# When the second layer's memory keys are split, in a two-layer hybrid encoder on one core

## The chip, the cores and the metric

The kernel runs on one core of one Trainium2 chip. The metric is the device time of one execution in microseconds. The kernel before takes 899.92 us (median of three runs, 897.84 to 900.17).

## What is computed

Two encoder layers over x of 256 x 2048. Each layer multiplies x by one wide input projection, runs three groups of heads, gates them and multiplies by an output projection; all in float32. The part that matters here is the memory attention and the two projections that follow its key projection in the program:

```python
h = x @ w_in
a_q, a_k, a_v, a_z, b_q, b_k, b_v, b_z, b_lr, m_q, m_z = jnp.split(h, cuts, axis=-1)
y_a = chunk_band_attention(heads_a(a_q), heads_a(a_k), heads_a(a_v), rel_table)
...
o_b = gla_chunk_recurrence(heads_k(b_q), heads_k(b_k), heads_v(b_v), heads_k(log_g))
...
mkv = mem @ w_mem_kv                      # mem: 256 tokens x 2048
mk, mv = jnp.split(mkv, 2, axis=-1)
y_m = memory_attention(heads_m(m_q), heads_m(mk), heads_m(mv))
...
y = jnp.concatenate([y_a * silu(a_z), y_b * silu(b_z), y_m * silu(m_z)], axis=-1)
x = layer_norm(DEEPNORM_ALPHA * x + y @ w_out, ln_g, ln_b)
```

## The kernel before

**Products in two parts.** A large product keeps float32 accuracy by splitting both operands into a rounded high part and the rest: `parts` (lines 126 to 129) rounds with a copy on ACT (ScalarE, line 128) and subtracts the rounded from the raw value on DVE (VectorE, line 129). PE (TensorE) then adds three products, high x high, low x high and high x low (`as_products`, lines 258 to 264).

**Weight pieces.** A projection of 512 columns (`as_group`, line 266) is done in 8 pieces of 256 rows. For each piece (`piece`, lines 140 to 158) SP issues the DMAs into `raw`, ACT makes `wh`, DVE makes `wl`, and PE does 12 matmuls of 512 columns. `raw`, `wh` and `wl` have 4 buffers each: the load of a piece waits until DVE has made the `wl` of the piece four places earlier, and a cast until PE is done with that piece.

**Turning.** Some results are needed with rows and columns exchanged. `turned` (from line 520) transposes 32 x 32 blocks on DVE (line 525), writes them to DRAM with a DMA issued by POOL (GpSimd; `home<-sc`, line 527), and two ticks later reads them back with 8 DMAs of POOL that put the blocks in place (`qk<-home`, line 532). What is then done to the turned tile is written in a `place` function, which `laid_out` hands to `placed`.

**Order of the work.** PE, SP and POOL run in the order of the program. After each 512-column piece `tick` moves a clock on by 1 and runs the generators on the list `side` whose time has come; a side generator that `laid_out` registers with 9 thus issues its instructions behind the ninth piece after the turning. On ACT and DVE a scheduler at build time orders the instructions, but the `place` instructions are pinned (`placed_here`): they keep their place in the program. Each engine takes its instructions one after the other, so one that waits holds all behind it.

**The place of the edit.** In the second layer the memory's values and keys (`G_MV`, `G_MK`) are projected first. The keys `acc` are turned into `raw` (a tile of the tag `qk`); then come the 8 pieces of `G_BQK` (queries and keys of the linear attention, line 863), `gla_inputs`, and `values(0, 512)`, a further 8 pieces (line 889). The `place` of the keys does two `parts` calls, so two casts on ACT and two subtractions on DVE, into `mk[0]` and `mk[1]`. They are read by `m_head` late in the layer. The result of `G_BQK` is turned in the same way, and lines 860 and 861 place it 9 pieces after that (`gq` on ACT, `gk` on DVE). Between the weight pieces DVE also scales and shifts the residual of the first layer (`restored`, lines 660 and 661, `res`).

Of the kernel before, what the change touches and what calls it, by code (L numbers as in the profile page):

```python
# [31 lines left out]
G_MK, G_MV, G_BQK, G_AQ0, G_AK0, G_AQ1, G_AK1, G_MQ, G_BZ, G_AZ0, G_AZ1, G_MZ, G_WO = range(13)  # L32
# [4 lines left out]
def hybrid_trunk_kernel(  # L37
# [12 lines left out]
    waiting, active, side, done, now, linear = [], [], [], set(), [0], []  # L50

    def tick(share=1.0):

        now[0] += share
        for e in [e for e in side if e[1] <= now[0]]:
            side.remove(e)
            after = next(e[0], None)
            if after is not None:
                side.append((e[0], now[0] + after))
            else:  # L60
                done.add(e[0])
        while True:
            while waiting and len(active) < (3 if all(g in done for g in linear) else 2):
                active.append((waiting.pop(0), 0))
            due = [e for e in active if e[1] <= now[0]]
            if not due:
                return
            active.remove(due[0])
            g = due[0][0]
            after = next(g, None)  # L70
            if after is not None:
                active.append((g, now[0] + after))
                return
            done.add(g)

    def finish(gens):
        while not all(g in done for g in gens):
            tick()
# [18 lines left out]
    def nm(s):  # L97
        uid[0] += 1
        return f"{s}_{uid[0]}"
# [17 lines left out]
    def operand():  # L117

        x = opp.tile([P, 4, 2, T], F32R, name=nm("x"), tag="x")
        return x[:, :, 0], x[:, :, 1], x.rearrange("p j h t -> p j (h t)")  # L120
# [5 lines left out]
    def parts(hi, lo, src, keep=lambda ins: ins):  # L126

        keep(act.copy(hi, src))  # L128
        keep(dve.tensor_tensor(lo, src, hi.bitcast(F32), op=ALU.subtract))  # L129

    def load_quarter(src):

        with tc.high_priority(AHEAD):
            raw = wp.tile([P, 4, T], F32, name=nm("raw"), tag="raw")
            x = operand()
            sp.dma_start(raw, src)
            parts(x[0], x[1], raw)
        return x

    def piece(src, n, kp=2, home=None):  # L140

        with tc.high_priority(AHEAD):
            raw = wp.tile([P, kp, n], F32, name=nm("raw"), tag="raw")
            if home is None:
                hi, lo = (wp.tile([P, kp, n], F32R, name=nm(w), tag=w) for w in ("wh", "wl"))
            else:
                hi, lo = home
            if isinstance(src, list):
                at = 0
                for part in src:  # L150
                    if len(part.shape) == 2:
                        part = part.rearrange("p (k n) -> p k n", k=kp)
                    sp.dma_start(raw[:, :, at:at + part.shape[2]], part)
                    at += part.shape[2]
            else:
                sp.dma_start(raw.rearrange("p k n -> p (k n)"), src)
            parts(hi, lo, raw)
        return hi, lo

    def resident_quarter(q, src):  # L160

        with tc.high_priority(AHEAD):
            x = operand()
            sp.dma_start(early[:, q], src)
            parts(x[0], x[1], early[:, q])
        return x
# [91 lines left out]
    def as_products(o, t, xq, w, kt, kk, first=0):  # L258
        wh, wl = w
        xh, xl, _ = xq[kt // 4]  # L260
        j, ts = kt % 4, slice(t * P, (t + 1) * P)
        mm(o, xh[:, j, ts], wh[:, kk], kt == first, False)
        mm(o, xl[:, j, ts], wh[:, kk], False, False)
        mm(o, xh[:, j, ts], wl[:, kk], False, kt == 15)

    def as_group(src, xq, n, kp=2, first=None, need={}):

        acc = psd.tile([P, 2, 512], F32, name=nm("acc"), tag="acc")
        for pc in range(16 // kp):
            if first is not None and pc % 2 == 0:  # L270
                xq.append(load_quarter(first[pc // 2]))
            finish(need.get(pc, ()))
            w = piece(src[pc], n, kp)
            for kk in range(kp):
                for t in range(2):
                    as_products(acc[:, t, :n], t, xq, w, pc * kp + kk, kk)
            tick(n / 512)
        return acc
# [232 lines left out]
    def placed(raw, place):  # L511

        if place is not None:
            for t in range(2):
                place(raw[:, t].rearrange("p a (g j) -> p g a j", j=32),
                      lambda x: x[:, :, t * P:(t + 1) * P].rearrange("p g (a j) -> p g a j", j=32))
        return
        yield

    def turned(n, *todo, order="p b (g j) -> p g b j"):  # L520

        homes = []
        for _, src in todo:
            blocks = scratch([P, 4, n])
            dve.transpose(blocks.rearrange(order, j=32), src.rearrange("p (g b j) -> p g b j", b=4, j=32))  # L525
            homes.append(drm.tile([P, 4, n], F32, name=nm("home"), tag=f"home{n}"))
            pool.dma_start(homes[-1], blocks)  # L527

        def reads():
            for (dst, _), home in zip(todo, homes):  # L530
                for b in range(4):
                    pool.dma_start(dst[b * 32:(b + 1) * 32], home[:, b].rearrange("(a i) n -> i a n", a=4))  # L532
            return
            yield

        side.append((reads(), now[0] + 2))
# [118 lines left out]
    def restored(gb):  # L655

        for n in range(WO_N):
            for t in range(2):
                r = res[:, t, columns(n)]
                tc.keep_in_program_order(dve.tensor_tensor(r, r, gb[n][0], op=ALU.mult))  # L660
                dve.tensor_tensor(r, r, gb[n][1], op=ALU.add)
                yield 2
# [4 lines left out]
    def wo_pieces(l, n):  # L667

        if n < 3:
            return [w512[l, G_WO + n, pc] for pc in range(8)]  # L670
        return [[w256[l, i, pc // 2][:, pc % 2 * 512:pc % 2 * 512 + 512] for i in range(2)] for pc in range(8)]
# [143 lines left out]
    for l in range(L):  # L815
        def halves(g):
            return [[w512[l, g, h * 4 + pc // 2][:, pc % 2 * 512:pc % 2 * 512 + 512] for h in range(2)] for pc in range(8)]

        def staged(g, x, raw, place):
            return laid_out(as_group(halves(g), x, 512), raw, place)  # L820

        def laid_out(acc, raw, place):
            raw = raw.rearrange("p (t a) n -> p t a n", t=2) if raw.shape[2] == P else raw.rearrange("p (t a) (b n) -> p t (a b) n", t=2, n=P)
            turned(P, *((raw[:, t], acc[:, t]) for t in range(2)))
            gen = placed(raw, place)
            side.append((gen, now[0] + (6 if place is None else 9)))
            return [gen]

        mk = [per.tile([P, 4, T], F32R, name=nm("mk"), tag=f"mk{i}") for i in range(2)]
        mv = [per.tile([P, 2, 512], F32R, name=nm("mv"), tag=f"mv{i}") for i in range(2)]  # L830
        xq = []
        if l == 0:
            def each(p):
                if p in (2, 4, 6, 7):
                    xq.append(resident_quarter(len(xq), xT[len(xq)]))

            raw = hd.tile([P, 4, T], F32, name=nm("qk"), tag="qk", bufs=4)
            laid_out(first_memory(mv, each), raw, lambda src, at: parts(at(mk[0]), at(mk[1]), src, placed_here))
        else:
            memq = []  # L840
            parts(*mv, as_group(w512[l, G_MV], memq, 512, 2, memT))
            gens = [transposed(xq, gbT), restored(gb)]
            waiting.append(gens[0])

            def rest():
                for q, xT in turns.items():
                    xq.append(operand())
                    yield from landed(xq[q], xT, q, gbT[1])

            side.append((rest(), now[0] + 6))  # L850
            raw = hd.tile([P, 4, T], F32, name=nm("qk"), tag="qk", bufs=4)
            mkey = staged(G_MK, memq, raw, lambda src, at: parts(at(mk[0]), at(mk[1]), src, placed_here))
            finish(gens[:1])

        gq = hd.tile([P, 2, T], F32, name=nm("gq"), tag="gq")
# [1 line left out]
        raw = hd.tile([P, 4, T], F32, name=nm("qk"), tag="qk", bufs=4)  # L857
# [5 lines left out]
        acc = as_group(halves(G_BQK), xq, 512)  # L863
# [97 lines left out]
        acc = as_group(halves(G_BZ), xq, 512)  # L961
# [6 lines left out]
        for i, g in ((1, G_AZ0), (2, G_AZ1), (3, G_MZ)):  # L968
            acc = as_group(halves(g), xq, 512)
# [22 lines left out]
        for n in range(WO_N):  # L992
# [3 lines left out]
            src = wo_pieces(l, n)  # L996
# [141 lines left out]
```

## Time and profile before

| | |
|---|---|
| timed runs, median (range) | 899.92 us (897.84 to 900.17) |
| profiled execution, its own time | 899.75 us |
| its span in the trace | 898.0 us |
| PE busy | 889.1 us, 99% |
| PE weight loads (PEld) busy | 743.6 us, 83% |
| DVE busy | 613.7 us, 68% |
| ACT busy | 478.0 us, 53% |
| POOL busy | 230.9 us, 26% |

A timeline row has the start and the duration in us, the engine, the line in the code, the operation, the tiles as out<-in, shapes, the number of instructions that were merged, and in brackets how long the engine was idle before it and what ended that time. "DMA qk<-home" there means that the landing of that transfer did. SPq is SP's queue of DMA issues; the time of a transfer from issue to landing stands apart from it. In the rows of a stretch, each engine has its busy time with the number of its instructions in parentheses; then come the granted TensorE clock, the share of the 16 DMA engines that is busy, and GB/s.

### The profile page before, as it was taken

The page shows a single profiled execution, that of the slowest core. Times are in us where ns is not written, and L with a number is a line of the kernel's source. Part 1 is how long each engine was busy: PE and PEld are TensorE (multiplying, and loading weights), DVE is VectorE, ACT ScalarE, POOL GpSimd, SP SyncE. Part 2 cuts the span into 40 slices and gives each one's busy share as a digit, 9 for nine tenths or more (in the row PEclk, how much of TensorE's full clock was granted, in tenths as well). Part 3 has the DMA queues.
Part 4 walks back from the last instruction along what each step waited for, and adds up shares of the span by engine and source line. Part 5 has one row for each costly group of instructions (what it writes and reads, how often), then busy time and mean ns, then how long its engine had stood idle before and what let it go on. Part 6 is the DMA issues. An engine that isn't in the chain of part 4 may idle for free.

```text
span 898.0 us, 13829 instructions
## 1 busy us (share of the span) xinstructions
PE 889.1 (99%) x4663; PEld 743.6 (83%) x4663; DVE 613.7 (68%) x893; ACT 478.0 (53%) x686; POOL 230.9 (26%) x431
## 2 busy tenths in 40 slices
PE   9999999999999999999999999999999999999997
PEld 7888988888988888888888788888888888888885
DVE  6766568757477666665595687896565758676766
ACT  6643574555446565543465544754744457565440
POOL 0022103114315353410033221231061334342300
PEclk9999999999999999999999999999999999999998
DMA  9987779967989797975689879697489887978752
GB/s 301 318 264 223 223 244 263 272 195 226 266 259 242 238 279 228 297 254 193 225 267 270 229 203 291 192 290 219 144 235 290 244 265 232 271 237 275 219 183 93
DMA packets 166086, 216.88 MB, mean 242 GB/s; under 512 B 25232, under 2 KB 143376, under 8 KB 166016
## 3 DMA queue, kind: packets, MB, share of 16 engines
q1 hardware_dynamic: 148256, 173.29, 63.7%
q0 software_dynamic: 17472, 42.33, 16.2%
q8 instruction: 36, 0.59, 0.3%
q10 hardware_dynamic: 288, 0.39, 0.1%
q14 instruction: 34, 0.28, 0.1%
HBM read 194.78 MB, written 21.10 MB: 240 GB/s over the span
## 4 chain that ended last, share of the span: by engine, by line
PE 71%; issue 13%; DMA 9%; DVE 3%; POOL 2%; ACT 1%; SPq 0%; DVEq 0%; POOLq 0%; ACTq 0%
PE acc L102 65%; PE bk L102 6%; DMA zT<-home 2%; DMA home<-sc 2%; DMA xT<-home 2%; DMA raw<-w 2%; DVE wl L129 1%; DMA qk<-home 1%; DMA res<-memT 1%; DMA gb<-ln_b 1%; POOL home L527 0%; POOL xT L532 0%; DMA pT<-home 0%; POOL qk L532 0%; DVE sc L525 0%
## 5 line engine op out<-in xcount | busy, mean ns | idle before, releaser
L102 PE MATMUL acc<-wh,x 128*128 128x512 f32 (+2 forms) x2516 | 748.4, 381 | 0.2 <-ACT wh L128 0.2
L102 PEld LDWEIGHTS acc<-wh,x 128*128 128x128 f32 x2516 | 460.9, 188 | 87.1 <-ACT wh L128 1.0
L129 DVE TENSOR_TENSOR wl<-raw,wh 128x1024 fp32r<-128x1024 f32 (+3 forms) x321 | 368.0, 1151 | 203.0 <-ACT wh L128 196.8
L128 ACT CAST wh<-raw 128x1024 fp32r<-128x1024 f32 (+3 forms) x321 | 318.1, 995 | 336.5 <-PE acc L102 185.7
L102 PE MATMUL acc<-wl,x 128*128 128x512 f32 (+2 forms) x1258 | 476.3, 379 | 1.4 <-DVE wl L129 1.3
L102 PEld LDWEIGHTS acc<-wl,x 128*128 128x128 f32 x1258 | 236.0, 188 | 48.1 <-DVE wl L129 3.5
L527 POOL DMA_DIRECT2D home<-sc x76 | 42.5, 560 | 436.0 <-DVE sc L525 423.1
L532 POOL DMA_DIRECT2D pT<-home x96 | 52.4, 552 | 24.8 <-PE acc L102 8.8
L532 POOL DMA_DIRECT2D qk<-home x64 | 34.9, 553 | 35.5 <-DMA home<-sc 25.2
L532 POOL DMA_DIRECT2D zT<-home x48 | 26.1, 551 | 19.0 <-DMA home<-sc 13.4
L525 DVE STREAM_TRANSPOSE sc<-sc 128x512 f32<-128x512 f32 (+1 forms) x38 | 24.9, 667 | 3.7 <-ACT sc L974 3.0
L532 POOL DMA_DIRECT2D yr<-home x48 | 26.3, 555 | 4.2 <-DMA home<-sc 3.2
L554 ACT ACTIVATE sc<-sc,mx 128x128 f32<-128x128 f32 (+1 forms) x32 | 14.4, 449 | 13.0 <-DVE mx L552 13.0
L525 DVE STREAM_TRANSPOSE sc<-acc 128x512 f32<-128x512 f32 x28 | 18.3, 690 | 4.4 <-PE acc L102 4.3
L547 DVE SCALAR_TENSOR_TENSOR sc<-bk,bias 128x384 f32<-128x384 f32 x16 | 8.6, 538 | 10.8 <-PE bk L102 10.8
L128 ACT CAST x<-sc 128x512 fp32r<-128x512 f32 x20 | 12.3, 618 | 5.3 <-DVE sc L508 2.7
L532 POOL DMA_DIRECT2D xT<-home x24 | 13.2, 552 | 6.5 <-DMA xT<-home 5.3
L129 DVE TENSOR_TENSOR x<-sc,x 128x512 fp32r<-128x512 f32 x20 | 13.5, 684 | 1.4 <-ACT x L128 1.4
L102 PEld LDWEIGHTS bk<-pT,asv 128*128 128x128 f32 x64 | 11.8, 189 | 1.8
L102 PE MATMUL bk<-qk,qk 128*128 128x128 f32 (+1 forms) x64 | 13.1, 326 | 0.0
L676 DVE SCALAR_TENSOR_TENSOR res<-res,acc 128x512 f32<-128x512 f32 x15 | 9.6, 681 | 5.0 <-PE acc L102 5.0
L102 PE MATMUL bk<-pT,asv 128*128 128x256 f32 (+1 forms) x64 | 13.0, 326 | 0.0
(208 smaller groups left out, 508.6 us busy)
## 6 DMA issues: line engine op xcount, KB each, us to landing
raw<-w SPq DMA_DIRECT2D x387, 256.0 KB, 4.6
raw<-w SPq DMA_DIRECT2D x62, 512.0 KB, 4.5
home<-sc POOLq DMA_DIRECT2D x60, 256.0 KB, 4.4
raw<-w SPq DMA_DIRECT2D x32, 388.0 KB, 5.0
raw<-w SPq DMA_DIRECT2D x32, 264.0 KB, 3.5
qk<-home POOLq DMA_DIRECT2D x64, 64.0 KB, 5.4
raw<-w SPq DMA_DIRECT2D x32, 124.0 KB, 4.9
bias<-relw SPq DMA_DIRECT2D x16, 192.0 KB, 4.3
```

The source lines that it names most:

```text
L102: pe.matmul(o, l, r, start=start, stop=stop, skip_group_check=True)
L128: keep(act.copy(hi, src))
L129: keep(dve.tensor_tensor(lo, src, hi.bitcast(F32), op=ALU.subtract))
L525: dve.transpose(blocks.rearrange(order, j=32), src.rearrange("p (g b j) -> p g b j", b=4, j=32))
L527: pool.dma_start(homes[-1], blocks)
L532: pool.dma_start(dst[b * 32:(b + 1) * 32], home[:, b].rearrange("(a i) n -> i a n", a=4))
L547: dve.scalar_tensor_tensor(s, pb[:, :384], SCALE, bias[h], op0=ALU.mult, op1=ALU.add)
L554: act.activation(s[:, own[t]], s[:, own[t]], AF.Exp, bias=mx[:, t:t + 1], accum_out=zs[:, t:t + 1])
L676: dve.scalar_tensor_tensor(r, r, ALPHA, acc, op0=ALU.mult, op1=ALU.add)
```

## The change

`staged` and `laid_out` get a parameter `later`, 9 unless given, and the second layer's key projection gives 12. The first layer's keys go through `laid_out` directly and keep 9, as do all others.

```diff
-        def staged(g, x, raw, place):
-            return laid_out(as_group(halves(g), x, 512), raw, place)
-
-        def laid_out(acc, raw, place):
+        def staged(g, x, raw, place, later=9):
+            return laid_out(as_group(halves(g), x, 512), raw, place, later)
+
+        def laid_out(acc, raw, place, later=9):
             raw = raw.rearrange("p (t a) n -> p t a n", t=2) if raw.shape[2] == P else raw.rearrange("p (t a) (b n) -> p t (a b) n", t=2, n=P)
             turned(P, *((raw[:, t], acc[:, t]) for t in range(2)))
             gen = placed(raw, place)
-            side.append((gen, now[0] + (6 if place is None else 9)))
+            side.append((gen, now[0] + (6 if place is None else later)))
             return [gen]
...
-            mkey = staged(G_MK, memq, raw, lambda src, at: parts(at(mk[0]), at(mk[1]), src, placed_here))
+            mkey = staged(G_MK, memq, raw, lambda src, at: parts(at(mk[0]), at(mk[1]), src, placed_here), 12)
```

What this does to the order of ACT, in the second layer: the last piece of `G_BQK` (`wh_892`) and the first four of `values(0, 512)` (`wh_908`, `wh_911`, `wh_914`, `wh_917`). Of the two numbers behind a name the first is the same before and after; the second is a serial number.

```order
 L128 CAST wh_892_4833<-raw_891_4832 128x1024
 L128 CAST wh_908_4881<-raw_907_4880 128x1024
+L128 CAST wh_911_4902<-raw_910_4901 128x1024
+L128 CAST wh_914_4929<-raw_913_4928 128x1024
+L128 CAST wh_917_4950<-raw_916_4949 128x1024
 L128 CAST mk_784_4273<-qk_821_4468 128x4x128 x2
-L128 CAST wh_911_4906<-raw_910_4905 128x1024
-L128 CAST wh_914_4933<-raw_913_4932 128x1024
-L128 CAST wh_917_4954<-raw_916_4953 128x1024
 L128 CAST wh_920_4973<-raw_919_4972 128x1024
 L300 CAST gw_900_4864<-gwraw_901_4865 48x256
```

The two casts of the keys stood between the first and the second piece, and stand now between the fourth and the fifth.

On DVE at the same place, first where the subtractions leave (`acc_865` is the result of `G_BQK`, whose transposes follow):

```order
 L129 TENSOR_TENSOR wl_893_4834<-raw_891_4832,wh_892_4833 128x1024
 L129 TENSOR_TENSOR wl_909_4882<-raw_907_4880,wh_908_4881 128x1024
-L129 TENSOR_TENSOR mk_785_4274<-qk_821_4468,mk_784_4273 128x4x128 x2
 L660 TENSOR_TENSOR res_102<-res_102,gb_758_4207 128x512
-L129 TENSOR_TENSOR wl_912_4907<-raw_910_4905,wh_911_4906 128x1024
 L661 TENSOR_TENSOR res_102<-res_102,gb_758_4207 128x512
-L129 TENSOR_TENSOR wl_915_4934<-raw_913_4932,wh_914_4933 128x1024
+L129 TENSOR_TENSOR wl_912_4903<-raw_910_4901,wh_911_4902 128x1024
+L129 TENSOR_TENSOR wl_915_4930<-raw_913_4928,wh_914_4929 128x1024
 L660 TENSOR_TENSOR res_102<-res_102,gb_758_4207 128x512
 L525 STREAM_TRANSPOSE sc_894_4851<-acc_865_4674 128x4x4x32
```

The subtractions are gone from here, and the scheduler has put one operation on `res` (line 661) ahead of the second piece's subtraction instead of behind it. Some rows further down, where they arrive:

```order
 L661 TENSOR_TENSOR res_102<-res_102,gb_758_4207 128x512
-L129 TENSOR_TENSOR wl_918_4955<-raw_916_4953,wh_917_4954 128x1024
+L129 TENSOR_TENSOR wl_918_4951<-raw_916_4949,wh_917_4950 128x1024
+L129 TENSOR_TENSOR mk_785_4274<-qk_821_4468,mk_784_4273 128x4x128 x2
 L867 TENSOR_TENSOR sc_898_4859<-acc_865_4674,sc_898_4859 128x512
 L129 TENSOR_TENSOR wl_921_4974<-raw_919_4972,wh_920_4973 128x1024
```

They stand behind the fourth piece's subtraction (`wl_918`), ahead of one operation on the linear attention's queries (line 867) and the fifth piece's subtraction. Two further operations on `res` change places with a neighbouring `wl`. The orders of POOL, SP and PE are the same.

## Prediction

> **What bounds the kernel now.** I read the page's busy times first, then the list of what TensorE (PE) waited for, then the stretches around the edit, and last the timelines of each engine there. The first row says that PE is busy for all but 9 us of the span:
>
> ```profile
> PE 889.1 (99%) x4663; PEld 743.6 (83%) x4663; DVE 613.7 (68%) x893; ACT 478.0 (53%) x686; POOL 230.9 (26%) x431
> ```
>
> Of the five rows in which PE waited for another engine, these are the only two in which the weight stream held it (in all, times, longest, in us):
>
> ```profile
> PE acc L102 <- DVE wl L129: 1.3, 3, 0.8
> ...
> PE acc L102 <- ACT wh L128: 0.2, 1, 0.2
> ```
>
> So nothing that ACT, DVE or the DMAs save counts unless it ends a PE wait, and the whole pool is about 1.5 us. The longest of these waits, 0.8 us, stands exactly where the edit works: PE's timeline at 514 us, then at 521 us.
>
> ```profile
> 513.93 0.39 PE L102 MATMUL acc<-wl,x 128*128 128x512 f32 x1
> ...
> 514.61 0.39 PE L102 MATMUL acc<-wl,x 128*128 128x512 f32 x1
> 514.84 0.70 PE L102 MATMUL acc<-wh,x 128*128 128x512 f32 x2
> 516.33 0.50 PE L102 MATMUL acc<-wl,x 128*128 128x512 f32 x1 [0.79 <-DVE wl L129]
> ...
> 517.13 0.39 PE L102 MATMUL acc<-wl,x 128*128 128x512 f32 x1
> ```
> ```profile
> 521.23 0.39 PE L102 MATMUL acc<-wl,x 128*128 128x512 f32 x1
> ...
> 522.20 0.50 PE L102 MATMUL acc<-wl,x 128*128 128x512 f32 x1
> ...
> 523.00 0.40 PE L102 MATMUL acc<-wl,x 128*128 128x512 f32 x1
> ```
>
> One `wl` matmul follows another after 0.68 us when nothing is late (514.61 - 513.93). The steps in the two places are 1.72, 0.80, 0.97 and 0.80 us instead, so PE loses 1.04 + 0.12 + 0.29 + 0.12 = **1.57 us** here. The "0.79" of the row is less than that because ends of matmuls are modelled; I use the starts.
>
> Why it is late is on ACT's timeline:
>
> ```profile
> 506.41 1.05 ACT L128 CAST wh<-raw 128x1024 fp32r<-128x1024 f32 x1 [2.36 <-DMA raw<-w]
> 509.46 0.62 ACT L128 CAST mk<-qk 128x512 fp32r<-128x512 f32 x1 [2.01 <-DMA qk<-home]
> 513.19 0.62 ACT L128 CAST mk<-qk 128x512 fp32r<-128x512 f32 x1 [3.10 <-DMA qk<-home]
> 513.71 3.90 ACT L128 CAST wh<-raw 128x1024 fp32r<-128x1024 f32 x4
> 521.05 0.41 ACT L300 CAST gw<-gwraw 48x256 fp32r<-48x256 f32 x1 [3.44 <-POOL gw L299]
> ```
>
> The two roundings of the keys wait for their readback, 2.01 and 3.10 us. Four weight casts queue behind the second and then run in one burst of 3.90 us. DVE has the same picture one step later; these are its rows up to 520 us and then up to 527:
>
> ```profile
> 507.49 1.23 DVE L129 TENSOR_TENSOR wl<-raw,wh 128x1024 fp32r<-128x1024 f32 x1 [2.19 <-ACT wh L128]
> ...
> 513.84 0.69 DVE L129 TENSOR_TENSOR mk<-qk,mk 128x512 fp32r<-128x512 f32 x1 [3.04 <-ACT mk L128]
> 514.45 0.68 DVE L660 TENSOR_TENSOR res<-res,gb 128x512 f32<-128x512 f32 x1
> 515.06 1.22 DVE L129 TENSOR_TENSOR wl<-raw,wh 128x1024 fp32r<-128x1024 f32 x1
> ...
> 518.53 1.31 DVE L525 STREAM_TRANSPOSE sc<-acc 128x512 f32<-128x512 f32 x2
> 519.76 0.65 DVE L866 COPY sc<-acc 128x512 f32<-128x512 f32 x1
> ```
> ```profile
> 522.06 0.68 DVE L867 TENSOR_TENSOR sc<-acc,sc 128x512 f32<-128x512 f32 x1
> 522.66 1.21 DVE L129 TENSOR_TENSOR wl<-raw,wh 128x1024 fp32r<-128x1024 f32 x1
> 524.40 0.68 DVE L869 TENSOR_REDUCE ms<-sc 128x8 f32<-128x512 f32 x1
> 525.11 0.42 DVE L301 TENSOR_TENSOR gw<-gwraw,gw 16x256 fp32r<-16x256 f32 x1
> ```
>
> The `wl` of 515.06 ends at 516.28, and PE goes on at 516.33: that is the wait. I name a weight piece by its `wh` tile, as the order rows do: this one is 911.
>
> **The change, part by part.** It adds and removes no instruction. Two casts on ACT (0.62 us each) and two subtractions on DVE (0.69 each) go from behind piece 908 to behind piece 917; POOL's and SP's rows keep their order. Moved work costs PE nothing by itself, but everything behind it shifts, so I follow the pieces through the new order.
>
> When the raw weights land is the other bound. SP's issues, and what a DMA of this tile took to land (between 500 and 523 us: least, median, most), with the wide half of piece 911 by itself:
>
> ```profile
> 502.96 1.19 SPq L153 DMA_DIRECT2D raw<-w  x2
> 504.25 1.21 SPq L153 DMA_DIRECT2D raw<-w  x2
> 508.74 1.20 SPq L153 DMA_DIRECT2D raw<-w  x2
> 516.30 1.19 SPq L153 DMA_DIRECT2D raw<-w  x2
> ```
> ```profile
> DMA to landing us min/median/max: 3.3/5.1/8.0
> ```
> ```profile
> raw<-w SPq DMA_DIRECT2D x1, 388.0 KB, 5.6
> ```
>
> Pieces 911 (502.96), 914 (504.25) and 920 (508.74) were under way while ACT stood still. Piece 911 had landed by about 509.1 (its second half starts at 503.5 and takes no longer than the first). The second part of 914 was issued at about 504.9; with the longest landing it is there by 512.9. Piece 917 lies between 914 and 920 in the queue; four casts without a gap from 513.71 put its landing at or before 515.6, and the longest landing from about 506.5 gives 514.5. For 920 the bound is 509.3 + 8.0 = 517.3.
>
> PE reaches 911 at 514.84 as before (12 matmuls a piece, 2.72 us) and asks for its `wl` 0.45 us into the piece. Without a wait it needs the low parts of 911, 914, 917, 920, 923 at 515.3, 518.0, 520.7, 523.5 and 526.2. The new order supplies:
>
> - **911**: cast 509.1 to 510.2 (1.05), subtraction to 511.4. 3.9 us early, where it was 1.0 late. On DVE two `res` operations (0.68 each) now stand ahead of it, in the idle time after 508.7.
> - **914**: cast to 514.0 at the latest, subtraction to 515.2. 2.8 us early.
> - **917**: cast to 515.6. On DVE a `res` operation, two transposes (1.31), a copy (0.65) and another `res` stand ahead of it: 515.2 + 0.68 + 1.31 + 0.65 + 0.68 + 1.22 = 519.7. 1.0 us early.
> - **920**: ACT does the two key casts first, 515.6 to 516.8, and finds their readback landed (513.2, as before), then casts 920 by 518.4. DVE: 519.7 + 2 x 0.69 + 0.68 + 1.21 = 523.0. 0.5 us early.
> - **923**: its transfer, issued at 516.30 when 911's subtraction had ended, now goes at 511.4; landed by 520.0, cast by 521.1. DVE: 523.0 + 0.68 + 0.68 + 0.42 + 1.22 = 526.0. 0.2 us early, by bounds that add up every longest value. With neighbours overlapping as in the rows (515.06 - 514.45 = 0.61, not 0.68) each is about 1 us better.
>
> So all 1.57 us go: the wait for 911 and its echo at 521 us, the wait for 917. The stall of the readback (5.1 us on ACT) has no successor there, because the casts come 2 us after it has landed. The keys themselves are read only much later:
>
> ```profile
> L102 PE MATMUL bk<-mk,mq x24: 279/282/285, 744.7 to 790.6; 128*128 128x256 f32 x24
> ```
>
> **Sum.** The profiled execution took 899.75 us, with a span of 898.0; 899.75 - 1.57 = **898.2**. The three timed runs are 897.84, 899.92 and 900.17, so the profiled one is close to their median. Bounds of the step: nothing gained, and 1.57 plus the rest of PE's waits on weights in the whole program, at most 2 us.
>
> **Rivals.**
>
> Partly taken: the DVE queue from 515 to 526 us is as full as before. The stretches (span, then PE, PEld, DVE, ACT, POOL busy, clock, DMA share, GB/s) say so:
>
> ```profile
> 510.00:515.00 5.00, 5.00 (x24) 3.98 (x23) 1.85 (x3) 1.90 (x4) 0.00 (x0) 1.00 0.93 248
> 515.00:520.00 5.00, 4.21 (x18) 3.17 (x19) 5.00 (x8) 2.61 (x3) 0.47 (x1) 1.00 0.47 116
> ```
>
> If 917 to 923 use up my margins of 0.2 to 1.0 us, up to half of the gain is lost again: 898.7 to 899.3. For it: two more subtractions ahead of 920's. Against it: DVE starts this stretch 3 us earlier.
>
> Nothing taken: the change doesn't do what it says to PE, because raw weights and not the keys bind, 899.7. Against it: 911 had landed 5 us before its cast.
>
> **Slower**: the same wait moves to the next readback. Lines 860 and 861 round nothing, but they too are pinned, wait for a readback of `qk`, and hold casts and subtractions behind them:
>
> ```profile
> 524.57 4.36 POOL L532 DMA_DIRECT2D qk<-home  x8 [3.30 <-ACT wh L128]
> ```
> ```profile
> 531.90 0.72 ACT L860 ACTIVATE gq<-qk 128x256 f32<-128x256 f32 x2
> ```
> ```profile
> DMA to landing us min/median/max: 3.0/3.5/4.0
> ```
>
> Here ACT found the data there. The weight stream, which stood still from 509.9 to 516.3, will be denser. The transposes end 2.6 us earlier (517.2 by the sum above, for 519.8), so the last of these reads is issued near 525.8 instead of 528.4, and lands at 529.3 with 3.5 us. ACT could come to line 860 at about 529, when PE has released the buffers of 923 (528.4) and one narrow cast is done. Queued behind it stand `wh` and, past two `res` operations on DVE, `wl` of the third narrow piece. PE wants that near 536.9 (923 starts at 525.7, two more wide pieces end at 533.9, two narrow ones with half the columns at 536.7). From landing to that `wl` it is an estimated 2.5 us (0.5 for the copies of line 861, 2 x 0.68, half of 1.22). A landing after 534.4 costs PE a microsecond for each of its own; after 536.0, which is a landing of 10.2 us, the kernel is slower than before. The longest landing above, 8.0, gives 533.8 and no loss, so this stays unlikely; with 12 us it is 901.6.
>
> The Trainium skill, "DMA: Bandwidth & Descriptors", section "Issuing engines are not separate DMA queues", says that transfers started by different engines run on the same 16 DMA engines and interleave. By that rule the earlier weight transfers would lengthen the readback, and the time would go towards this rival's 901.6. The trace agrees as far as direction goes: landings reach 8.0 us in the stretch with a DMA share of 0.93, against 4.0 here.
>
> More: an execution that stalled longer than the profiled one gains more, 897.
>
> **How the numbers follow.** Forecast 0.60; partly 0.12; nothing 0.08; slower 0.12, as much for what I overlook as for the readback; more 0.08. A measurement of this kernel can tell some 0.3%, 2.7 us, from no change, and the forecast's 1.57 is below it. With runs 2.3 us apart I give the forecast one chance in six to read beyond it: 0.10, and 0.05 from "more" make 0.15 for faster. Three quarters of "slower" would exceed it: 0.09. The rest, 0.76, is the same. The range: the forecast with the spread of the runs, about 1.8 below; above, the cases partly and nothing with a half microsecond: 896.4 to 900.3.
>
> **What would show it.** In the profile after: no `wl` step above 0.7 us between 513 and 524; ACT's two key casts without idle time ahead of them, near 515; SP's issue for 923 near 511.4; line 860 without a wait. Wrong: a key cast that still waits, a `PE acc <- DVE wl` row near 520 to 526, or ACT idle ahead of line 860.

## The result and the profile after

| | before | after |
|---|---|---|
| timed runs, median (range), 21 each | 899.36 us (897.36 to 903.12) | 897.52 us (896.86 to 900.45) |
| profiled execution, its own time | 899.75 us | 897.52 us |
| its span | 898.0 us | 895.8 us |

The ratio is 0.9982, with a 95% interval of 0.9974 to 0.9989: faster by 1.6 us of 899.4 (1.0 to 2.3 by the interval), and by less than 0.3%. The medians are 1.84 us apart. The spans are 2.2 us apart; where these come from is read off below.

PE's waits for the weight stream were two rows before, 1.3 and 0.2 us. In the profile after only the second is left:

```profile
PE acc L102 <- ACT wh L128: 0.2, 1, 0.2
```

PE's timeline after the change, at the second piece of `values(0, 512)` (911) and at the fourth (917). One `wl` matmul follows the other after 0.67 to 0.69 us, where the steps were 1.72, 0.80, 0.97 and 0.80 us:

```profile
514.00 0.39 PE L102 MATMUL acc<-wl,x 128*128 128x512 f32 x1
514.22 0.61 PE L102 MATMUL acc<-wh,x 128*128 128x512 f32 x2
514.67 0.39 PE L102 MATMUL acc<-wl,x 128*128 128x512 f32 x1
514.90 0.61 PE L102 MATMUL acc<-wh,x 128*128 128x512 f32 x2
515.36 0.39 PE L102 MATMUL acc<-wl,x 128*128 128x512 f32 x1
```
```profile
519.43 0.39 PE L102 MATMUL acc<-wl,x 128*128 128x512 f32 x1
519.66 0.61 PE L102 MATMUL acc<-wh,x 128*128 128x512 f32 x2
520.12 0.39 PE L102 MATMUL acc<-wl,x 128*128 128x512 f32 x1
```

When the starts of the same matmuls are set side by side, the profile after is 0.62 us ahead until 514 us (514.84 against 514.22) and 2.22 us ahead behind 521 us. So 1.60 us come from this place. Of the other 0.62, most is one wait in the first layer, which the change doesn't touch: before, a `wl` matmul came late by 0.37 us, and the next by 0.11.

```profile
151.37 0.61 PE L102 MATMUL acc<-wh,x 128*128 128x512 f32 x2
152.20 0.50 PE L102 MATMUL acc<-wl,x 128*128 128x512 f32 x1 [0.22 <-DVE wl L129]
152.53 0.63 PE L102 MATMUL acc<-wh,x 128*128 128x512 f32 x2
```

Both are from the execution before; in the one after the late step isn't there. One profile of each kernel must not be read as if all of their difference came from the edit.

ACT's timeline after the change. The row at 512.43 is both key casts: no bracket, so no idle time ahead of them. Three of the four weight casts that stood in the burst behind them (513.71 to 517.6 before) now stand ahead of them, 4 to 8 us earlier, and ACT's waits are now for PE, that is, for a free buffer:

```profile
506.03 1.06 ACT L128 CAST wh<-raw 128x1024 fp32r<-128x1024 f32 x1 [1.67 <-PE acc L102]
508.75 1.05 ACT L128 CAST wh<-raw 128x1024 fp32r<-128x1024 f32 x1 [1.66 <-PE acc L102]
511.47 1.06 ACT L128 CAST wh<-raw 128x1024 fp32r<-128x1024 f32 x1 [1.67 <-PE acc L102]
512.43 1.14 ACT L128 CAST mk<-qk 128x512 fp32r<-128x512 f32 x2
514.19 1.06 ACT L128 CAST wh<-raw 128x1024 fp32r<-128x1024 f32 x1 [0.62 <-PE acc L102]
515.15 0.40 ACT L300 CAST gw<-gwraw 48x256 fp32r<-48x256 f32 x1
...
528.33 0.72 ACT L860 ACTIVATE gq<-qk 128x256 f32<-128x256 f32 x2
```

The rows at 515.15 and 528.33 are two further instructions to look at: `gw`, which had 3.44 us of idle time ahead of it before, and line 860, which could have had to wait for its readback. Neither waits. DVE's row of the two key subtractions has none either:

```profile
514.11 1.22 DVE L129 TENSOR_TENSOR wl<-raw,wh 128x1024 fp32r<-128x1024 f32 x1
515.24 1.29 DVE L129 TENSOR_TENSOR mk<-qk,mk 128x512 fp32r<-128x512 f32 x2
516.44 0.69 DVE L867 TENSOR_TENSOR sc<-acc,sc 128x512 f32<-128x512 f32 x1
```

In the stretches (span; PE, PEld, DVE, ACT, POOL busy; clock; DMA share; GB/s) the DMAs have lost their gap: a share of 0.73 from 515 to 520 us, where it was 0.47, and DVE's work has moved ahead, 4.97 us from 510 to 515 where it was 1.85.

```profile
510.00:515.00 5.00, 5.00 (x24) 4.14 (x23) 4.97 (x7) 2.90 (x4) 1.69 (x4) 1.00 1.04 327
515.00:520.00 5.00, 5.00 (x24) 4.14 (x23) 4.94 (x9) 1.97 (x4) 2.75 (x6) 1.00 0.73 203
```

### The profile page after: what moved, and what is told of

Its sections match the earlier page's. It is cut to its first block, busy times and chain, and to the rows that moved or that the text cites. A ratio compares the mean times of both kernels' runs of the same rounds, so it can differ in the third digit from the quotient of the medians.

```text
span 895.8 us, 13828 instructions
## 1 busy us (share of the span) xinstructions
PE 888.2 (99%) x4663; PEld 743.9 (83%) x4663; DVE 614.3 (69%) x893; ACT 478.5 (53%) x686; POOL 230.8 (26%) x431
## 4 chain that ended last, share of the span: by engine, by line
PE 98%; DMA 0%; DVE 0%; ACT 0%; issue 0%
PE acc L102 92%; PE bk L102 6%; DMA raw<-w 0%; ACT res L801 0%; PE bk L643 0%; DVE stats L787 0%; DVE res L786 0%; ACT wh L128 0%; DVE res L737 0%; DVE mvt L740 0%; PE bk L790 0%; ACT nparts L791 0%; DVE rs_u L750 0%; DVE nt L754 0%; DVE nt L755 0%
## 5 line engine op out<-in xcount | busy, mean ns | idle before, releaser
L532 POOL DMA_DIRECT2D yT<-home x16 | 8.7, 549 | 16.5 <-DMA home<-sc 16.5
## 6 DMA issues: line engine op xcount, KB each, us to landing
raw<-w SPq DMA_DIRECT2D x62, 512.0 KB, 4.7
```

## The experiments

**Theory W**: the cost was the wait for the keys' readback, because the second piece's cast and subtraction were queued behind it with too little in hand. **Rival C**: it was crowding, four instructions too many ahead of the second piece. **Rival U**: the weight stream came late in that execution anyway, and the keys only stood there. "The place" is PE at pieces 911 to 917 of the second layer. Ratios are to the kernel before on the same chip, with 95% intervals.

| run | ratio | loss at the place in its profile |
|---|---|---|
| the change | 0.9982 (0.9974 to 0.9989) | none |
| other source at 9 | 0.9991 (0.9981 to 1.0000) | 0.35 us, at 522.7 us |
| the same again | 0.9986 (0.9973 to 0.9998) | none |
| extra work at 9, keys at 12 | 0.9987 (0.9974 to 1.0000) | none |
| keys at 10 | 0.9986 (0.9978 to 0.9995) | none |
| keys at 8 | 0.9997 (0.9987 to 1.0007) | none |
| the same again | 0.9999 (0.9988 to 1.0009) | none |
| first layer at 12 too | 0.9986 (0.9975 to 0.9997) | none |
| readback twice, keys at 12 | 0.9986 (0.9973 to 1.0000) | none |
| fills, keys at 9 | 1.0002 (0.9993 to 1.0011) | none, but 1.68 us ahead of it |
| fills, keys at 12 | 1.0060 (1.0042 to 1.0078) | none, but 6.20 us ahead of it |
| before, second and third profile | | 2.07 and 2.34 us |

### The kernel before, looked at again

Unchanged, twice.

> The kernel before, unchanged, for a second profile. Theory W: ACT waits for the readback with 2 to 6 us in all ahead of the key casts, and PE waits on the second piece's low part, with a loss that follows the landing (0.5 to 3 us). Rival U: ACT waits for raw weights instead in some executions, and the loss near 515 us is there without a wait at the keys.

> The kernel before once more, for a third profile: as for the second.

The two executions took 899.86 and 901.20 us. PE's wait is in the same place in both. The cast was late there as well, with 0.28 us of idle time on PE in the second profile and 0.54 in the third:

```profile
516.27 0.73 PE L102 MATMUL acc<-wh,x 128*128 128x512 f32 x2 [0.54 <-ACT wh L128]
517.79 0.50 PE L102 MATMUL acc<-wl,x 128*128 128x512 f32 x1 [0.78 <-DVE wl L129]
```

ACT waited 4.67 and 2.42 us for the readback in the second, 3.18 and 3.04 in the third, and each time a burst of four weight casts came behind the second wait (3.9 and 4.0 us). Set beside the profile after, the same matmuls fall behind by 2.07 and 2.34 us at the place; with 1.60 of the first profile that is 2.0 us in the mean. The loss is a habit of this kernel and no accident of one execution. That speaks against U. It also follows the landing: in all three profiles PE goes on 3.13 to 3.14 us after the second key cast begins (516.33 less 513.19, 516.43 less 513.30, 517.79 less 514.65).

### The wait taken away, the work left in place

Against the kernel before; the added parameter `other` is left out here.

```diff
-            gen = placed(raw, place)
+            gen = placed(raw if other is None else other, place)
...
-            mkey = staged(G_MK, memq, raw, lambda src, at: parts(at(mk[0]), at(mk[1]), src, placed_here))
+            mkey = staged(G_MK, memq, raw, lambda src, at: parts(at(mk[0]), at(mk[1]), src, placed_here), 9,
+                           mv[0].bitcast(F32).rearrange("p t (a n) -> p t a n", n=P))
```

> The second layer's two key casts and two subtractions stay at 9, in the same place of ACT's and DVE's order as in the kernel before, but read the high part of the memory's values, which has been there for 35 us, in place of the turned keys (so the second layer's memory attention uses values for keys). The readback is still made. Theory W (the wait for the readback's landing, with the weight casts queued behind it, is the cost): the ACT rows of the keys have no idle time, no PE wait on a low part near 515 and 521 us, and the time is that of the change, ratio to before 0.998 (some 1.6 us less). Rival C (not the wait but the crowding: four more instructions ahead of the second piece's cast and subtraction): the place is the same, so the time is that of before, ratio 1.000. Rival U (the second piece's raw weights come late, the keys only stand there): ratio 1.000 as well, with ACT waiting for raw weights in their place.

> The run with the other source at 9 once more (values for keys in the second layer's memory attention), since its first ratio, 0.9991 with 0.9981 to 1.0000, lies between the theories, and its profile had no wait at the keys but an echo of 0.3 us at 521 us. Theory W alone: 0.998. Wait and crowding together: 0.999 again, with a PE wait near 521 us and none near 515.

The first run came out between the theories, 0.9991; its profiled execution, 901.4 us, was the slowest of its twelve runs (the fastest 897.11). Raw weights of the third piece came late in it, ACT waited 2.83 us for them, and PE lost 0.35 us at 522.7 us; most of the rest was lost far from the place, 1.0 us near 49 us and 1.2 us at 149 to 153 us, both in the first layer. The second run gives 0.9986 and a profile without any loss at the place. ACT's rows in it; `mk<-mv` is the key casts with the other source, and nothing is held behind them:

```profile
504.55 1.05 ACT L128 CAST wh<-raw 128x1024 fp32r<-128x1024 f32 x1 [1.76 <-DMA raw<-w]
505.50 1.14 ACT L128 CAST mk<-mv 128x512 fp32r<-128x512 f32 x2
507.98 1.05 ACT L128 CAST wh<-raw 128x1024 fp32r<-128x1024 f32 x1 [1.35 <-DMA raw<-w]
```

The second interval holds W's 0.998; the first, which begins at 0.9981, only just holds the 0.9982 of the change. Only the first reaches C's 1.000. The order of the instructions was that of the kernel before, so taking the wait away does what moving the casts did, within these intervals.

### The work doubled, the wait left out

Against the kernel after, whose own key casts stay at 12:

```diff
+            early_keys = mv[0].bitcast(F32).rearrange("p t (a n) -> p t a n", n=P)
+            side.append((placed(early_keys, lambda src, at: parts(at(mk[0]), at(mk[1]), src, placed_here)), now[0] + 9))
```

> The change (12), and at 9 four further instructions: the two casts and two subtractions also run there on the high part of the values, as in the run with the other source, and are written over at 12. So the second layer does these four twice, and the crowded place of 9 is as full as in the kernel before, without a wait. Theory W (the wait): ratio to before 0.998, as the change alone, no PE wait near 515 us. Rival C (crowding): these 2.6 us of work on ACT and DVE hold the second piece back, 0.999 to 1.000.

0.9987, and PE's list of waits has one weight row of 0.3 us, which lies elsewhere: the starts of its matmuls keep a constant distance from the profile after from 50 us to the end. Four instructions more at 9 cost nothing that can be seen there. With the run before this one, C is out as the main cause; the interval leaves room for some tenths of a microsecond of it.

### One piece later is enough, one earlier is not

```diff
-            mkey = staged(G_MK, memq, raw, lambda src, at: parts(at(mk[0]), at(mk[1]), src, placed_here), 12)
+            mkey = staged(G_MK, memq, raw, lambda src, at: parts(at(mk[0]), at(mk[1]), src, placed_here), 10)
```

Against the kernel after; two further runs have 8 in the same place.

> The keys at 10: behind the second piece of values(0, 512) instead of the first (9) or the fourth (12). Theory W: ACT still waits for the readback, some 3 to 5 us, but only the third piece is held: its cast runs at 513.8 to 514.8, its subtraction ends by 516.1, and PE asks for it at 518.0. So the whole gain comes with this one step: ratio 0.998, ACT idle ahead of the key casts, no PE wait. Rival C: half of the gain at most, since the four instructions still stand in the crowded stretch: 0.999. Rival U: 1.000.

At 10 a wait is still there, shorter than the 3 to 5 us that were expected. ACT's rows: the second key cast waits 2.11 us and three weight casts follow in a burst.

```profile
509.17 1.05 ACT L128 CAST wh<-raw 128x1024 fp32r<-128x1024 f32 x1 [2.81 <-DMA raw<-w]
510.12 0.61 ACT L128 CAST mk<-qk 128x512 fp32r<-128x512 f32 x1
512.85 0.62 ACT L128 CAST mk<-qk 128x512 fp32r<-128x512 f32 x1 [2.11 <-DMA qk<-home]
513.38 2.95 ACT L128 CAST wh<-raw 128x1024 fp32r<-128x1024 f32 x3
```

PE has no wait between 500 and 530 us in this profile, and the ratio is 0.9986. What is held now is the third piece, which PE wants 2.72 us later. So it is not the wait that costs, but what stands behind it. By itself the profile is a weak test: this readback landed earlier than in the three profiles before. With the second piece behind it, PE would by the 3.13 us above have gone on near 515.98 (512.85 and 3.13), 0.4 us late (an estimate; PE asked at 515.60). The ratio is the firmer evidence.

> The keys at 8. The scheduler puts the first cast ahead of the first piece's cast and the second cast between the first and the second piece. Theory W: the first cast waits until about 509.5 and the first piece's cast ends near 511, an estimated 1 us before PE wants it; the second cast holds the second piece as in the kernel before. So ratio 1.000, at most 1.001. Rival C (crowding around the second piece): one cast and one subtraction have left that place, so a part of the gain, 0.999.

> The keys at 8 once more: its first ratio is 0.9997 (0.9987 to 1.0007), but its profile has no PE wait at the second piece, since the readback landed 1 us earlier than in the kernel before. Theory W: the second piece's cast is held by the second key cast as at 9, so an execution loses what the landing exceeds an estimated 512 us (in the time of the profile before); over many executions 0 to 2 us, ratio 0.999 to 1.000. If the second profile has no loss either and the ratio is 0.998, the place of the first cast, ahead of the first piece, is what makes 8 better than 9.

At 8 the ratios are 0.9997 and 0.9999: no gain, as W said. The profiles say something else. The readback had landed by 511.4 and 512.0 us, about 1 to 2 us before 513.2 of the profile before, and PE lost nothing at the place, though ACT waited 6.8 and 7.3 us in all for the keys. The second piece's low part was there an estimated 0.7 and 0.5 us before PE asked for it, so a landing later by that much would have cost time; whether that happened in the other runs isn't shown. The two profiled executions took 898.01 and 898.22 us, less than the medians of their kernels (898.56 and 898.79). Why the runs without a profile are slower than these two is not settled.

### The first layer too

```diff
-            laid_out(first_memory(mv, each), raw, lambda src, at: parts(at(mk[0]), at(mk[1]), src, placed_here))
+            laid_out(first_memory(mv, each), raw, lambda src, at: parts(at(mk[0]), at(mk[1]), src, placed_here), 12)
```

Against the kernel after.

> The change, and the first layer's keys at 12 as well. In the first layer the two key casts of the kernel before have no idle time ahead of them (65.58 us), and PE waits for no weights there. Theory W: no difference from the change, ratio to before 0.998. Rival C: moving them out of the first layer's stretch gives a further 0.001 to 0.002.

0.9986, and the end of its trace is 0.2 us from that of the change: no difference. Where the casts had no wait, there was nothing to win.

### A later readback

First by ten and sixteen fills of the target by POOL ahead of the readback:

```diff
         def reads():
+            for _ in range(fills):
+                for dst, _ in todo:
+                    pool.memset(dst, 0.0)
```

> As the kernel before (9), with ten fills of the target tile by POOL (128x512 each, 0.53 us in the trace) between the write of the turned keys and their readback, so that the readback starts an estimated 2 to 3 us later. The scheduler, which counts the fills, puts the first cast between the first and the second piece, and the second between the third and the fourth. Theory W counts what is queued behind a wait, not how long it is: the second piece is held until an estimated 512 to 513 and its low part ends by 515, so PE loses 0 to 0.5 us; ratio 0.998 to 0.999, although the readback lands later and ACT waits as long. A plain reading of the wait (each microsecond of a later landing is a microsecond lost) gives 1.002 to 1.003.

> As the change (12), with sixteen such fills (some 8.5 us), so that the readback lands an estimated 5 us later, near 516 to 518 us. Theory W: ACT waits 3 to 5 us at the key casts again, now behind the fourth piece; the fifth piece is cast by an estimated 519.5 and PE wants it at 522.4 (in the time of the profile after). So no loss: ratio to before 0.998, with ACT idle ahead of the key casts and no PE wait. If a wait at this place costs what it cost at 9, the ratio is 1.001 to 1.003.

Both times came out otherwise, 1.0002 and 1.0060, and not for a reason that either expectation had. The fills themselves did it, 13 us ahead of the place. In the run with sixteen, two small DVE operations, which take 0.72 us together in the kernel before (there line 623), stood from 495.76 to 502.62, and the fills end at 502.15:

```profile
495.76 6.86 DVE L626 TENSOR_SCALAR sc<-xT,gbT 128x256 f32<-128x256 f32 x2
```
```profile
494.60 7.55 POOL L532 MEMSET qk<- 128x512 f32 x16
```

PE then waited 3.18 us for a `wl`. At the place itself neither run lost anything. In the run with sixteen fills the readback had landed when ACT came to it, so that it tells nothing about a wait at 12. In the run with ten, 1.68 us were lost at 501 us and the 1.6 of the place won, which fits its 1.0002; ACT waited 1.07 us at the first key cast, which the scheduler had put behind the first piece, and the second cast stood behind the third piece. So the run with ten fills fits W's reading of the place, the run with sixteen doesn't test it, and the times say nothing for or against it.

Then by making the readback twice:

```diff
-            for (dst, _), home in zip(todo, homes):
+            for (dst, _), home in list(zip(todo, homes)) * times:
```

> The change (12), with the keys' readback made twice in a row, the second after the first has landed, so that the keys are there an estimated 5 to 7 us later (518 to 520 us). The scheduler puts the casts behind the fourth and the fifth piece. Theory W with cover (a wait costs only what the pieces behind it do not have in hand): ACT waits 2 to 5 us for the readback again, the pieces behind are wanted 4 us later, and PE does not wait: ratio 0.998 to 0.999. If a wait of this length costs wherever it stands, 1.000 to 1.003.

ACT waits again at 12:

```profile
513.67 1.05 ACT L128 CAST wh<-raw 128x1024 fp32r<-128x1024 f32 x1 [1.93 <-DVE res L660]
516.85 0.62 ACT L128 CAST mk<-qk 128x512 fp32r<-128x512 f32 x1 [2.12 <-DMA qk<-home]
518.29 1.05 ACT L128 CAST wh<-raw 128x1024 fp32r<-128x1024 f32 x1 [0.82 <-DVE mk L129]
519.47 0.62 ACT L128 CAST mk<-qk 128x512 fp32r<-128x512 f32 x1
```

PE waits for none of it; the ratio is 0.9986. In the profile after, all of the keys had landed by 511.0 us (the last DMA of the readback was issued at 504.0, and none took more than 7.0). Here the first half landed at 516.8 and the second by 519.5, and that costs nothing at 12.

## Why the prediction held

The forecast was 898.2 us, made of 899.75 less 1.57; the median is 897.52.

- **The size.** 1.57 us of late steps at the place were read from the starts of the matmuls; 1.60 went there, and the ratio's 1.6 us agree. The list of waits alone (0.8 us in its row) would have given half. That the three agree so closely is in part luck: the other two profiles of the kernel before lost 2.07 and 2.34 us there, and the interval allows 1.0 to 2.3. Of the 0.7 us between forecast and median, 0.4 is the start: the profiled execution took 899.75, the median is 899.36.
- **The chances** put 1.57 us below what a measurement of this kernel can tell from no change. With 21 runs of each kernel the interval leaves 1.000 out, so it could be told.
- **The mechanism**, a wait that holds the weight casts queued behind it, is shown from two sides: without the wait and with the work the gain is there, and with the wait but another piece behind it as well. The pair of profiles before and after would not show it alone: the keys had landed by 511.0 us in the execution after, 2.1 us earlier than before, so that with the keys at 9 PE would have had the second piece's low part near 514.2 (an estimate, by the 3.13 us), ahead of the 514.67 at which it asked. The run with the readback made twice has the late landing: its first key cast began at 516.85, and PE lost nothing.
- **The echo at 521 us** went with it, as forecast.
- **Piece by piece** the forecast was too late. It had the second piece's cast at 509.1, from the landing of its raw weights in the execution before; it ran at 506.03. The stream of the execution after was ahead already at 490 us, where nothing is changed: the weight cast of 489.41 before ran at 487.36, and from 500.59 on ACT waited for PE and not for raw weights. The same cast differs by 2 to 3 us between executions: it ran at 507.27 in the run with the first layer at 12, and at 509.17, when its raw weights had landed, in the run with the keys at 10. SP's issue for 923 was expected at 511.4 and came at 508.4, for the same reason (516.30 before).
- **The margins** of 0.2 to 1.0 us at 917 to 923, added up from longest values, were larger in this execution: in the rows above 917's subtraction ends at 515.33 (514.11 + 1.22), and PE asks for its result at 520.12, so 4.8 us were in hand where the sum had 1.0. The rival "partly" finds no loss to stand on in any profile with the keys at 12.
- **Slower**, the wait that moves to line 860, did not come: the readback there took 2.1 to 3.6 us to land, where the rival needed 10.2. It had taken 3.0 to 4.0 before. The rule of the Trainium skill that the prediction set beside it ("DMA: Bandwidth & Descriptors", section "Issuing engines are not separate DMA queues": transfers of all engines share 16 DMA engines and interleave) gives a direction and no size. The weight stream was denser from 510 to 515 us (a DMA share of 1.04, 0.93 before), but a little thinner while this readback ran: 0.77 from 517.2 to 523.9 us, against 0.81 from 524.5 to 531.9 before. The prediction had held long weight transfers against short readbacks. Readbacks alone agree with the rule in direction: those of the keys, in the profile before, took 3.9 to 6.9 us at a share of 0.95.
- **More**: the executions before lose 1.6 to 2.3 us at this place, so some gain more than the profiled one. The runs after lie closer together (eleven of 21 within 897.23 and 897.86, one at 900.45).

## What to carry to other kernels

An instruction that is pinned into an in-order queue costs nothing while it waits, if what stands behind it isn't wanted yet; it costs from the microsecond at which its successor is late. So price such a wait by the successor's due time, not by its own length: in single profiles 2.1 us of it cost nothing one piece further on and 7.3 us in all cost nothing where the keys landed early enough, while 2.4 us ahead of the second piece cost 2.1. Read the loss from the steps between matmul starts, and look at a second profile of the unchanged kernel before a difference of spans is put down to an edit.

## What the runs showed of the hardware

**POOL's fills stop DVE.** The two `TENSOR_SCALAR` of 128x256 that took 0.72 us stood 6.86 us while POOL filled 128x512 tiles, and 4.06 us beside ten fills (497.12 to 501.18, the fills until 500.71). The first of the pair was held (6.54 us in the run with sixteen) and ended just behind the last fill. A `TENSOR_TENSOR` at 495.16, beside the first fills, took its usual 0.68 us, so not every DVE operation stops. What these rows can't show is the mode that DVE was in. The Trainium skill, "SBUF — State Buffer", section "Who interferes with whom", says that a DVE operation in a mode that uses two ports, which `tensor_scalar` can be in, and a GpSimd operation exclude each other for the whole of an instruction. The stops agree with it in kind; that DVE got no turn between one fill and the next is more than the section says.

**The clock drops after one long PE wait.** PE's timeline in the run with sixteen fills, and its stretches:

```profile
500.02 0.61 PE L102 MATMUL acc<-wh,x 128*128 128x512 f32 x2
503.81 0.80 PE L102 MATMUL acc<-wl,x 128*128 128x512 f32 x1 [3.18 <-DVE wl L129]
504.40 1.05 PE L102 MATMUL acc<-wh,x 128*128 128x512 f32 x2
505.26 0.63 PE L102 MATMUL acc<-wl,x 128*128 128x512 f32 x1
```
```profile
500.00:505.00 5.00, 1.82 (x6) 1.19 (x5) 5.00 (x6) 2.61 (x4) 2.74 (x6) 0.78 0.07 17
505.00:510.00 5.00, 5.00 (x14) 3.90 (x13) 4.17 (x4) 2.42 (x3) 3.81 (x7) 0.54 0.92 256
```

A group of three matmuls takes 1.45 us behind the gap (505.26 less 503.81), where it takes 0.68 otherwise, and the granted clock of the stretch is 0.54; from 502.8 to 509.6 us alone it is 0.50. Of the 6.20 us that this run lost here, the step across the wait is 3.3 (503.81 less 500.02, less 0.46 for the two matmuls between), so about 2.9 are the slow clock. The wait of 1.4 us in the run with ten fills left the clock at 1.00. So this wait of 3.2 us cost nearly twice its own time, and the one of 1.4 us didn't; each was seen in one profile, and where between them the clock begins to drop isn't shown.

**POOL's first readback.** In every profile POOL stands idle 2.3 to 2.5 us between the first and the second DMA of the keys' readback, and the profile names nothing that it waits for; after the change it reads

```profile
500.71 3.80 POOL L532 DMA_DIRECT2D qk<-home  x7 [2.53 <-issue]
```

What it is stays open. In the kernel before it is 2.5 of the 17 us that the keys took from the issue of their write (495.71) to their landing (513.1).
